# A hybrid decoder trunk on one core: embedding projections moved between mixer and MLP, two first tiles in token halves instead of four, TensorE's order there written by hand

## The chip, the cores and the metric

The kernel runs on one core of one Trainium2 chip. The metric is device time in microseconds (us) of one execution. The engines of the core are TensorE (PE, with its weight loads as PEld), VectorE (DVE), ScalarE (ACT), GpSimd (POOL, all but unused here) and the sync engine (SP), which issues the DMAs.

## The reference, cut to what matters

512 tokens of 1024 features run through two layers. A layer is a token mixer (Mamba-2 SSD in layer 0, HGRN2 in layer 1), a squared-ReLU MLP and a gated embedding; the first two are added to a scaled input and normalized.

```python
def sq_relu_mlp(h, w1, w2):
    a = jax.nn.relu(h @ w1)
    return (a * a) @ w2
...
        h = layer_norm(DEEPNORM_ALPHA * x + mix, ln_g[i, 0], ln_b[i, 0])
        h = layer_norm(DEEPNORM_ALPHA * h + sq_relu_mlp(h, mlp_w1[i], mlp_w2[i]), ln_g[i, 1], ln_b[i, 1])
        x = h + jax.nn.sigmoid(h @ ple_w_gate[i]) * (p[i] @ ple_w_proj[i])
```

`mix` is the output of the layer's mixer, which ends in a product with its output weights. p has 256 features per token and layer, so the embedding projection p @ ple_w_proj (wp in the kernel) is a quarter of the gate's matmul h @ ple_w_gate (wg), and it depends on neither h nor the mixer.

## The kernel before, in words

**Arithmetic.** Everything is float32, done in three passes: each operand is split into a rounded high part and the rest (`whi`, `wlo` for weights: a ScalarE cast and a VectorE subtraction, `split`, L110 and L112), and `mm3` issues high x high, high x low and low x high (L116, L117, L118) into one PSUM bank. Weights come in units of 128x1024 (512 KB) through three `raw` buffers; their loads stand on the sync queue.

**Tiles.** The 512 tokens are four chunks of 128. The residual stream `acc` lies in SBUF with tokens on partitions; projections need features on partitions, so each chunk is normalized, transposed by TensorE (`transpose_split`, L230: four transposes into bank pt, four into pm), copied by ScalarE (high part, L235) and VectorE (low part, L236).

**Order.** Python code issues the work, and a scheduler orders each engine's line by priorities; `tc.high_priority` moves a piece forward. Inside `tc.manual_schedule` TensorE's line is as the code is written. Each engine takes up its line in order, and the engines meet at semaphores.

**Mixer's end.** `out_project` multiplies the mixer's output by the last four weight units, chunk by chunk, two parts of 12 matmuls per chunk (one for each 512 output features; a part in the timeline is one bank `pj`). VectorE evicts each part into `acc` (L250 in layer 0, L252 in layer 1), and behind a chunk's second part stand its norm (`after`, L204 to L221: statistics, L220 subtracts the mean, L221 scales) and its transposes (`turned`). In layer 0 the eviction needs a scale per token: squares of the mixer's output are added up (`ss`), and `rms_group` sums them over features by small matmuls against ones (L721), a root and a reciprocal. In layer 1, HGRN's last two heads go through an output norm ahead of out_project: ScalarE squares sums of the core's result (L1117, L1120), VectorE scales it (L1122, L1126), TensorE transposes it (L1135, one group pt and one pm), ScalarE and VectorE split it (L1136, L1137). Out_project's first inner products need the heads before; the last ones need these.

**MLP.** `mlp_and_gate` runs five periods: T is a tile of 128 hidden features (24 matmuls, ReLU and square on ScalarE), Q a block product with w2 in Strassen's form (sums of w2 units, L323 to L329). The first period is eight T. In its first four tiles the first 256 tokens are multiplied for all four tiles before the second 256, so that the third and fourth chunk's norms have time. The last period is seven Q; behind its parts stand the second norm and the first chunk's transposes.

**Gates.** The rest of `mlp_and_gate` goes through two halves of 512 output features and four chunks each. In the first half all four chunks' projections p @ wp are made first (6 matmuls each, four banks), with turned(1) among them; then each chunk's gate (24 matmuls), a sigmoid on ScalarE, the product with the projection from PSUM (L486) and the addition to acc (L489). turned(2) and turned(3) stand inside the first and second chunk's gate. In the second half each chunk's projection stands in front of its gate.

Of the kernel before, what the change touches and what calls it, by code (L numbers as in the profile page):

```python
# [31 lines left out]
PERIODS = ("TTTTTTTT",) + 3 * ("TTQTQTQTQTQTQTQ",) + ("QQQQQQQ",)  # L32
# [9 lines left out]
def trunk(ctx: ExitStack, tc, a):  # L42
# [215 lines left out]
    def out_project(w, xs, first, after=None, turned=None, sums=None, scale=None):  # L258


        if after is not None:
            units = [unit(w[i]) for i in range(4)]
            for c in range(NCH):
                for h in range(2):
                    out_part(units[2 * h : 2 * h + 2], 4, xs, c, h, first, scale, True, sums)
                after(c)
                turned(c)
# [114 lines left out]
    def mlp_and_gate(layer, h_s, last):  # L382
# [4 lines left out]
        def hidden(g):  # L387
# [5 lines left out]
            for p in range(2):  # L393
                tiles = [4 * (2 * g + r) + 2 * p + i for r in range(2) for i in range(2)]
                us = []
                if g == p == 0:
                    for m in tiles:
                        us.append((unit(w1[m]), bank(psj, "pj")))
                        project(us[-1][0], h_s, us[-1][1], tok=slice(0, 256))
                zs = []  # L400
                for r in range(2):
                    z = mk(w4, [P, 2, T], "ab"[r])
                    for i in range(2):
                        if us:
                            u, ps = us[2 * r + i]
# [11 lines left out]

        for g, period in enumerate(PERIODS):
            if g < 4:
                tiles = hidden(g)  # L420
            if g > 0:
                if g == 4:
                    h_s, after, turned, sums = norm(2 * layer + 1)
                    p_s = (mk(w4, [P, 2, T], "a", F32R), mk(w4, [P, 2, T], "b", F32R))
                    praw = mk(raws, [P, 1024], "raw")
                    nc.sync.dma_start(praw, a[f"pT_{layer}"].rearrange("p k t -> p (k t)"))
                    praw = praw.rearrange("p (k t) -> p k t", k=2)
                    nc.scalar.copy(p_s[0], praw)
                    nc.vector.tensor_sub(p_s[1], praw, f32(p_s[0]))
# [19 lines left out]
        pps = {}  # L449

        def proj(c, pu):

            pp = pps[c] = bank(*((psj, "pj") if c > 1 and pps else (psy, "py%d" % (c % 2))))
            for k in range(2):
                ks = slice(k * 512, (k + 1) * 512)
                mm3(pp, p_s[0][:, k, c * P : (c + 1) * P], p_s[1][:, k, c * P : (c + 1) * P], pu[0][:, ks], pu[1][:, ks], k == 0, k == 1)

        for h in range(2):
            pu = unit(a[f"wp_{layer}"][h])
            gu = [unit(a[f"wg_{layer}"][4 * h + j]) for j in range(4)]  # L460
            for c in range(NCH):
                sl = slice(c * P, (c + 1) * P)
                if h == c == 0:
                    for i in range(NCH):
                        proj(i, pu)
                        if i == 1:
                            turned(1)
                if h == 1:
                    proj(c, pu)
# [813 lines left out]
```

## Time and profile before

| | |
|---|---|
| median of 3 runs | 1422.53 us (1421.46 to 1422.73) |
| profiled execution, its own time | 1422.3 us |
| its span, first to last instruction | 1420.5 us |
| mean granted TensorE clock | 1.000 |
| TensorE busy | 1413.6 us, 8143 matmul records |
| VectorE busy | 1025.4 us (72%) |
| ScalarE busy | 744.4 us (52%) |
| DMA | 174.83 MB, mean 123 GB/s |

In the page's list of engines each busy time is followed by its share of the span and the number of instructions. A timeline row gives the start in the span, the duration, the engine, the line of the code, the operation and its tiles (out<-in, shape; xN groups N that follow one another), and in brackets an idle time of the engine just before, with what ended it. Matmul rows overlap: the next one starts before the last one ends. In the list of waits a row says which instruction waited for which, the time in all, how often, and the longest.

### The profile page before, as it was taken

The page shows a single profiled execution, that of the slowest core. Times are in us where ns is not written, and L with a number is a line of the kernel's source. Part 1 is how long each engine was busy: PE and PEld are TensorE (multiplying, and loading weights), DVE is VectorE, ACT ScalarE, POOL GpSimd, SP SyncE. Part 2 cuts the span into 40 slices and gives each one's busy share as a digit, 9 for nine tenths or more (in the row PEclk, how much of TensorE's full clock was granted, in tenths as well). Part 3 has the DMA queues.
Part 4 walks back from the last instruction along what each step waited for, and adds up shares of the span by engine and source line. Part 5 has one row for each costly group of instructions (what it writes and reads, how often), then busy time and mean ns, then how long its engine had stood idle before and what let it go on. Part 6 is the DMA issues. An engine that isn't in the chain of part 4 may idle for free.

```text
span 1420.5 us, 20454 instructions
## 1 busy us (share of the span) xinstructions
PE 1413.6 (100%) x8143; PEld 1182.3 (83%) x8143; DVE 1025.4 (72%) x1713; ACT 744.4 (52%) x1089; POOL 1.6 (0%) x9
## 2 busy tenths in 40 slices
PE   9999999999999999999999999999999999999998
PEld 7888888888888888888888888888898888888887
DVE  7987777778967667677963774776785867667873
ACT  7776656664265454545543446465454544544641
POOL 0000000000000000000000000000000000000000
PEclk9999999999999999999999999999999999999999
DMA  8343333233433444442422222222163444444231
GB/s 292 127 145 108 113 118 101 95 104 124 158 119 127 156 133 149 134 148 104 149 90 91 92 92 72 90 90 76 60 238 104 148 147 135 149 133 163 89 119 45
DMA packets 48960, 174.83 MB, mean 123 GB/s; under 512 B 5728, under 2 KB 6368, under 8 KB 48736
## 3 DMA queue, kind: packets, MB, share of 16 engines
q1 hardware_dynamic: 48864, 173.52, 35.9%
q8 instruction: 64, 1.05, 0.3%
q14 instruction: 32, 0.26, 0.1%
HBM read 171.34 MB, written 2.16 MB: 122 GB/s over the span
## 4 chain that ended last, share of the span: by engine, by line
PE 96%; DVE 2%; DMA 1%; ACT 0%; issue 0%; SPq 0%
PE pj L116 25%; PE pj L118 25%; PE pj L117 25%; PE py L116 5%; PE py L118 5%; PE py L117 5%; PE py L687 1%; PE py L942 1%; PE pm L669 1%; PE py L689 1%; PE pt L635 0%; PE pt L230 0%; DMA acc<-in_xw 0%; PE pm L230 0%; DVE wlo L112 0%; DVE b L236 0%
## 5 line engine op out<-in xcount | busy, mean ns | idle before, releaser
L110 ACT CAST whi<-raw 128x1024 fp32r<-128x1024 f32 x226 | 237.1, 1050 | 377.8 <-PE pj L117 264.6
L112 DVE TENSOR_TENSOR wlo<-raw,whi 128x1024 fp32r<-128x1024 f32 x226 | 274.3, 1220 | 159.1 <-ACT whi L110 155.0
L116 PE MATMUL pj<-b,whi 128*128 128x512 f32 (+1 forms) x1008 | 381.5, 379 | 0.2 <-ACT b L235 0.2
L117 PE MATMUL pj<-b,whi 128*128 128x512 f32 (+1 forms) x1008 | 379.4, 376 | 0.7 <-DVE b L236 0.7
L118 PE MATMUL pj<-b,wlo 128*128 128x512 f32 (+1 forms) x1008 | 378.9, 376 | 0.0
L118 PE MATMUL pj<-whi,b 128*128 128x512 f32 (+1 forms) x592 | 229.5, 388 | 0.0
L116 PE MATMUL pj<-whi,b 128*128 128x512 f32 (+1 forms) x584 | 229.3, 393 | 0.0
L117 PE MATMUL pj<-wlo,b 128*128 128x512 f32 (+1 forms) x584 | 226.1, 387 | 0.0
L116 PEld LDWEIGHTS pj<-b,whi 128*128 128x128 f32 x1008 | 189.5, 188 | 36.2 <-issue 1.7
L118 PEld LDWEIGHTS pj<-b,wlo 128*128 128x128 f32 x1008 | 189.8, 188 | 34.7
L117 PEld LDWEIGHTS pj<-b,whi 128*128 128x128 f32 x1008 | 189.8, 188 | 34.6 <-DVE b L236 0.9
L118 PEld LDWEIGHTS pj<-whi,b 128*128 128x128 f32 x592 | 111.3, 188 | 22.9 <-DVE b L1137 0.2
L116 PEld LDWEIGHTS pj<-whi,b 128*128 128x128 f32 x584 | 109.8, 188 | 22.7 <-ACT k L871 0.5
L117 PEld LDWEIGHTS pj<-wlo,b 128*128 128x128 f32 x584 | 109.8, 188 | 21.2
L110 ACT CAST whi<-r 128x1024 fp32r<-128x1024 f32 x64 | 67.4, 1053 | 63.8 <-PE pj L118 35.6
L112 DVE TENSOR_TENSOR wlo<-r,whi 128x1024 fp32r<-128x1024 f32 x64 | 78.0, 1219 | 22.2 <-ACT whi L110 22.0
L118 PE MATMUL py<-whi,b 128*128 128x512 f32 x216 | 84.2, 390 | 0.0
L117 PE MATMUL py<-wlo,b 128*128 128x512 f32 x192 | 74.8, 389 | 0.0
L116 PE MATMUL py<-whi,b 128*128 128x512 f32 x192 | 74.4, 389 | 0.0
L573 DVE SCALAR_TENSOR_TENSOR cv<-pj,cst,cv 128x509 f32<-128x509 f32 (+2 forms) x66 | 49.0, 742 | 8.7 <-ACT cv L570 8.4
L118 PEld LDWEIGHTS py<-whi,b 128*128 128x128 f32 x216 | 40.5, 188 | 8.5
L116 PEld LDWEIGHTS py<-whi,b 128*128 128x128 f32 x192 | 36.1, 188 | 7.6
(321 smaller groups left out, 1816.0 us busy)
## 6 DMA issues: line engine op xcount, KB each, us to landing
raw<-in_w SPq DMA_DIRECT2D x112, 512.0 KB, 3.2
r<-in_w SPq DMA_DIRECT2D x64, 512.0 KB, 3.5
raw<-in_wssd SPq DMA_DIRECT2D x38, 512.0 KB, 3.7
a<-csd SPq DMA_DIRECT2D x16, 512.0 KB, 3.5
raw<-in_wso SPq DMA_DIRECT2D x16, 512.0 KB, 3.4
raw<-in_wg SPq DMA_DIRECT2D x16, 512.0 KB, 3.4
raw<-in_whvg SPq DMA_DIRECT2D x16, 512.0 KB, 3.3
raw<-in_whq SPq DMA_DIRECT2D x16, 512.0 KB, 3.4
```

The costliest lines, as they stand in the source:

```text
L110: nc.scalar.copy(hi[:, :n], f)
L112: nc.vector.tensor_sub(lo[:, :n], f, f32(hi[:, :n]))
L116: nc.tensor.matmul(out, sh, mh, start=start, stop=False, **kw)
L117: nc.tensor.matmul(out, sh, ml, start=False, stop=False, **kw)
L118: nc.tensor.matmul(out, sl, mh, start=False, stop=stop, **kw)
L573: nc.vector.scalar_tensor_tensor(cv[:, d:], ps[:, : T - d], convw[:, i, k : k + 1], cv[:, d:], ALU.mult, ALU.add)
L669: nc.tensor.matmul(pst_[:, c * P : (c + 1) * P], btok[:, c, :], xw[:, c].rearrange("p h q -> p (h q)"), start=True, stop=True)
L687: nc.tensor.matmul(yd[64 * r : 64 * r + 64, sl], xdt[:, c, r, :], m[:, r, sl], start=True, stop=c == 0)
L689: nc.tensor.matmul(yd[64 * r : 64 * r + 64, sl], pv[:, c - 1, r, :], ecs[:, r, (c - 1) * P : c * P], start=False, stop=True,)
L942: nc.tensor.matmul(ps[r][32 * b : 32 * b + 32, base + n * c : base + n * c + n], kk[r][:, ts], moving(r, 4 * c + b), start=True, stop=True,)
```

## The change

- A new function `embed` computes all eight projections of a layer (two feature halves, four chunks, 6 matmuls each) between out_project and the MLP. ScalarE copies each bank to SBUF (`blk`), and two DMAs of 1 MB per layer store them to DRAM (`ple`). The gates read them back in four loads per layer. The loads of p and wp have a high priority.
- The transposes of chunks 2 and 3 stand later: turned(0) and turned(1) come behind the first part of chunks 2 and 3 in out_project, turned(2) between embed's two halves, and turned(3) behind the first half tile of the MLP.
- Two tiles, not four, are done in token halves. The first of the tiles' steps is taken ahead of the periods, so the first period has one T less.
- out_project of both layers, embed and the first tiles are in a manual schedule for TensorE. rms_group is called where out_project's arguments are made, so its matmuls (L732 now) stand ahead of all of out_project's.
- The gates begin without projections; the transposes of chunks 1, 2 and 3 stand inside the gates of the chunk ahead, at k = 4 of 8.

```diff
-PERIODS = ("TTTTTTTT",) + 3 * ("TTQTQTQTQTQTQTQ",) + ("QQQQQQQ",)
+PERIODS = ("TTTTTTT",) + 3 * ("TTQTQTQTQTQTQTQ",) + ("QQQQQQQ",)
...
                     out_part(units[2 * h : 2 * h + 2], 4, xs, c, h, first, scale, True, sums)
+                    if h == 0 and c > 1:
+                        turned(c - 2)
                 after(c)
-                turned(c)
...
+    def embed(layer, turned):
+
+        with tc.high_priority(offset=2 * LEAD):
+            p_s = (mk(w4, [P, 2, T], "a", F32R), mk(w4, [P, 2, T], "b", F32R))
+            praw = mk(raws, [P, 1024], "raw")
+            nc.sync.dma_start(praw, a[f"pT_{layer}"].rearrange("p k t -> p (k t)"))
+            praw = praw.rearrange("p (k t) -> p k t", k=2)
+            nc.scalar.copy(p_s[0], praw)
+            nc.vector.tensor_sub(p_s[1], praw, f32(p_s[0]))
+        for h in range(2):
+            pu = unit(a[f"wp_{layer}"][h], 2 * LEAD)
+            out = tmp("blk", [P, NCH, T])
+            for c in range(NCH):
+                pp = bank(psj, "pj")
+                for k in range(2):
...
+                    mm3(pp, p_s[0][:, k, cs], p_s[1][:, k, cs], pu[0][:, ks], pu[1][:, ks], k == 0, k == 1)
+                nc.scalar.copy(out[:, c], pp)
+            nc.sync.dma_start(a["ple"][layer, h], out.rearrange("p c t -> p (c t)"))
+            if h == 0:
+                turned(2)
...
-                    for m in tiles:
+                    for m in tiles[:2]:
                         us.append((unit(w1[m]), bank(psj, "pj")))
                         project(us[-1][0], h_s, us[-1][1], tok=slice(0, 256))
+                        if len(us) == 1:
+                            early_turned(3)
...
+        early_turned = turned
+        tiles = hidden(0)
+        with tc.manual_schedule(engines={mybir.EngineType.PE}):
+            embed(layer, turned)
+            next(tiles)
...
+        pp = []
+        for c in range(NCH):
+            pp.append(tmp("r", [P, 2, T]))
+            nc.sync.dma_start(pp[c], a["ple"][layer, :, :, c * T : (c + 1) * T].rearrange("h p t -> p h t"))
...
-                        if h == 0 and c < 2 and k == 2:
-                            turned(c + 2)
+                        if h == 0 and c < 3 and k == 4:
+                            turned(c + 1)
...
-                    nc.vector.tensor_mul(sg[:, cs], pp[:, cs], sg[:, cs])
+                    nc.vector.tensor_mul(sg[:, cs], pp[c][:, h, cs], sg[:, cs])
...
-    out_project(a["wso"][12:16], ys[3], False, *after, scale=rms_group(3, bank(psm, "pm")))
+    with tc.manual_schedule(engines={mybir.EngineType.PE}):
+        out_project(a["wso"][12:16], ys[3], False, *after, scale=rms_group(3, bank(psm, "pm")))
```

The line of each engine shows where instructions have moved. Up to the end of layer 0's mixer TensorE's line is the same. There, in the line of before, out_project's first part (bank pj_3179) is begun behind the last part of the mixer's pieces (pj_3120), and eleven of its twelve matmuls stand ahead of the sum of squares (L721):

```order
L117 MATMUL pj_3120<-wlo_3020,b_336_1982 128x512
L118 MATMUL pj_3120<-whi_3018,b_337_1983 128x512
L116 MATMUL pj_3179<-whi_3157,b_468_2744 128x512
L117 MATMUL pj_3179<-wlo_3159,b_468_2744 128x512
L118 MATMUL pj_3179<-whi_3157,b_469_2745 128x512
```

These are its first rows, and its end is this:

```order
L117 MATMUL pj_3179<-wlo_3165,b_468_2744 128x512
L118 MATMUL pj_3179<-whi_3163,b_469_2745 128x512
L116 MATMUL pj_3179<-whi_3163,b_468_2744 128x512
L117 MATMUL pj_3179<-wlo_3165,b_468_2744 128x512
L721 MATMUL pm_3143<-ones_s_169,ss_2751 64x64 x8
L118 MATMUL pj_3179<-whi_3163,b_469_2745 128x512
```

After the change the sum of squares, now L732, stands directly behind pj_3120:

```order
L117 MATMUL pj_3120<-wlo_3020,b_336_1982 128x512
L118 MATMUL pj_3120<-whi_3018,b_337_1983 128x512
L732 MATMUL pm_3145<-ones_s_169,ss_2751 64x64 x8
L116 MATMUL pj_3181<-whi_3159,b_468_2744 128x512
L117 MATMUL pj_3181<-wlo_3161,b_468_2744 128x512
L118 MATMUL pj_3181<-whi_3159,b_469_2745 128x512
```

The eleven matmuls have moved behind it. At the same place, VectorE's line before, with the sums of squares (L715) of the last two tiles as its first and its seventh row:

```order
L715 TENSOR_TENSOR ss_2751<-ss_2751,sq_3080 128x512
L250 SCALAR_TENSOR_TENSOR acc_99<-pj_3083,ri_2741,acc_99 128x512
L705 SCALAR_TENSOR_TENSOR y_3112<-xs_2884,cst_165,py_530_3097 128x512
L706 TENSOR_TENSOR y_3112<-y_3112,sz_2955 128x512
L112 TENSOR_TENSOR wlo_3406<-raw_3402,whi_3404 128x1024
L709 SCALAR_TENSOR_TENSOR b_469_2745<-y_3112,cst_165,b_468_2744 128x512
L715 TENSOR_TENSOR ss_2751<-ss_2751,sq_3117 128x512
L250 SCALAR_TENSOR_TENSOR acc_99<-pj_3120,ri_2741,acc_99 128x512
```

And after (the line L726 is the sum):

```order
L726 TENSOR_TENSOR ss_2751<-ss_2751,sq_3080 128x512
L250 SCALAR_TENSOR_TENSOR acc_99<-pj_3083,ri_2741,acc_99 128x512
L391 TENSOR_TENSOR b_3373<-raw_3374,a_3372 128x1024
L716 SCALAR_TENSOR_TENSOR y_3112<-xs_2884,cst_165,py_530_3097 128x512
L717 TENSOR_TENSOR y_3112<-y_3112,sz_2955 128x512
L112 TENSOR_TENSOR wlo_3382<-raw_3378,whi_3380 128x1024
L720 SCALAR_TENSOR_TENSOR b_469_2745<-y_3112,cst_165,b_468_2744 128x512
L112 TENSOR_TENSOR wlo_3436<-raw_3432,whi_3434 128x1024
L726 TENSOR_TENSOR ss_2751<-ss_2751,sq_3117 128x512
L250 SCALAR_TENSOR_TENSOR acc_99<-pj_3120,ri_2741,acc_99 128x512
```

Two instructions have come ahead of the last sum: the split of p (L391) and the split of the second wp unit (L112 for wlo_3436). ScalarE's cast of that unit has likewise moved ahead of the square sq_3117, which stood in front of a cast before. Further down, VectorE's order now has the eviction of the sixth part (pj_3287) ahead of chunk 1's L220, L204 and L221; before, chunk 1's L221 stood ahead of the eviction of the sixth part.

The second place is the end of HGRN in layer 1. In TensorE's line before, 14 of out_project's matmuls (banks pj_9027, pj_9069, pj_9083) stand between the mixer's last matmul (L1113) and the first transposes (L1135), and four up to the second ones:

```order
L117 MATMUL pj_9069<-wlo_8993,b_1243_7734 128x512
L118 MATMUL pj_9069<-whi_8991,b_1244_7735 128x512
L116 MATMUL pj_9083<-whi_9003,b_1243_7734 128x512
L117 MATMUL pj_9083<-wlo_9005,b_1243_7734 128x512
L1135 MATMUL pt_8965<-cst_165,qo_8929 128x128 x4
L118 MATMUL pj_9083<-whi_9003,b_1244_7735 128x512
L116 MATMUL pj_9083<-whi_9003,b_1243_7734 128x512
L117 MATMUL pj_9083<-wlo_9005,b_1243_7734 128x512
L118 MATMUL pj_9083<-whi_9003,b_1244_7735 128x512
L1135 MATMUL pm_8966<-cst_165,qo_8930 128x128 x4
L116 MATMUL pj_9013<-whi_8997,b_1243_7734 128x512
```

After, where L1125 is the mixer's last matmul and L1147 the transposes:

```order
L1123 MATMUL pm_8906<-b_1238_7653,sc_6356 128x128
L1125 MATMUL pm_8906<-xc_8892,qt_8562 128x128
L1147 MATMUL pt_8943<-cst_165,qo_8907 128x128 x4
L116 MATMUL pj_8993<-whi_8977,b_1249_7712 128x512
L1147 MATMUL pm_8944<-cst_165,qo_8908 128x128 x4
L117 MATMUL pj_8993<-wlo_8979,b_1249_7712 128x512
L118 MATMUL pj_8993<-whi_8977,b_1250_7713 128x512
L116 MATMUL pj_8993<-whi_8977,b_1249_7712 128x512
L117 MATMUL pj_8993<-wlo_8979,b_1249_7712 128x512
```

None of out_project's matmuls is left ahead of the first transposes, and one between the two groups; what follows are the last five of the first part (pj_8993), whose inputs b_1249 and b_1250 are the split of these transposes.

The third place is the entry of layer 0's gates (layer 1's is alike). TensorE's line before, from the last product of the MLP (bank py_927) over the first chunk's transposes (pt_5868) to the projections:

```order
L117 MATMUL py_927_5611<-wlo_5854,blk_4978 128x512
L118 MATMUL py_927_5611<-whi_5852,blk_4978 128x512
L230 MATMUL pt_5868<-cst_165,acc_99 128x128 x4
L230 MATMUL pm_5869<-cst_165,acc_99 128x128 x4
L116 MATMUL pj_5986<-whi_5930,a_5568 128x512
L117 MATMUL pj_5986<-wlo_5932,a_5568 128x512
L118 MATMUL pj_5986<-whi_5930,b_5569 128x512
L116 MATMUL pj_5986<-whi_5930,a_5568 128x512
```

After, up to the first gate (bank pj_5998, with b_923 and b_925 as the high and low split of the chunk):

```order
L118 MATMUL py_943_5649<-whi_5890,blk_5022 128x512
L116 MATMUL py_943_5649<-whi_5890,blk_5022 128x512
L230 MATMUL pt_5906<-cst_165,acc_99 128x128 x4
L230 MATMUL pm_5907<-cst_165,acc_99 128x128 x4
L117 MATMUL py_943_5649<-wlo_5892,blk_5022 128x512
L118 MATMUL py_943_5649<-whi_5890,blk_5022 128x512
L116 MATMUL pj_5998<-whi_5976,b_923_5607 128x512
L117 MATMUL pj_5998<-wlo_5978,b_923_5607 128x512
L118 MATMUL pj_5998<-whi_5976,b_925_5609 128x512
```

The transposes stand two matmuls earlier, and the gate, which stood behind 24 projection matmuls, now stands behind two.

39 lines of the change are left out of this document (11 added, 28 removed).

## Prediction

> **What bounds the kernel now.** I read the shares of the engines and the chain that ended last, then the list of TensorE's waits, then the timeline at the places that the change touches.
>
> ```profile
> PE 1413.6 (100%) x8143; PEld 1182.3 (83%) x8143; DVE 1025.4 (72%) x1713; ACT 744.4 (52%) x1089; POOL 1.6 (0%) x9
> ...
> PE 96%; DVE 2%; DMA 1%; ACT 0%; issue 0%; SPq 0%
> ```
>
> The chain that ended last is TensorE for 96% of the span, and TensorE is busy for all of it. So a microsecond counts only where TensorE comes to stand: work of VectorE, ScalarE or a queue costs nothing as long as TensorE has matmuls in line.
>
> ```profile
> PE pj L117 <- DVE b L236: 0.7, 1, 0.7
> ...
> PE pj L116 <- ACT b L235: 0.2, 1, 0.2
> ```
>
> Of the few waits that the list has, these two lie where the change cuts. The timeline puts both at the entry of layer 0's MLP, where the second token halves begin right behind the last transposes (L230):
>
> ```profile
> 384.39 0.28 PE L117 MATMUL pj<-b,whi 128*128 128x256 f32 x1
> 384.51 0.28 PE L118 MATMUL pj<-b,wlo 128*128 128x256 f32 x1
> ...
> 385.06 0.60 PE L230 MATMUL pm<-cst,acc 128*128 128x128 f32 x4
> ...
> 387.31 0.39 PE L117 MATMUL pj<-b,whi 128*128 128x256 f32 x1 [0.67 <-DVE b L236]
> 387.54 0.28 PE L118 MATMUL pj<-b,wlo 128*128 128x256 f32 x1
> ```
>
> Half matmuls (256 tokens) start 0.12 us apart (384.39, 384.51). A first matmul follows a group of transposes by 0.36 (1009.29 and 1009.65 below). Without a wait the matmul at 387.54, the sixth behind the transposes, would start at 385.06 + 0.36 + 5 x 0.12 = 386.02: this stretch can give back 1.5 us.
>
> Elsewhere TensorE's line is never empty. A row shows 0.39 us for a 128x512 matmul, but they overlap; the pitch comes from starts. Eleven steps lie between 347.53 and 350.02 below: 2.49 / 11 = 0.227 us.
>
> **Term 1: layer 0, the sum of squares** (L721 before, L732 after). Now eleven matmuls of out_project stand ahead of it and cover the work on its input. After the change it stands ahead of them all.
>
> ```profile
> 347.53 0.39 PE L118 MATMUL pj<-whi,b 128*128 128x512 f32 x1
> ...
> 350.02 0.39 PE L117 MATMUL pj<-wlo,b 128*128 128x512 f32 x1
> 350.34 0.69 PE L721 MATMUL pm<-ones_s,ss 128*64 128x64 f32 x16
> ```
>
> ```profile
> 348.15 0.62 ACT L711 ACTIVATE sq<-y 128x512 f32<-128x512 f32 x1
> 348.67 1.03 ACT L110 CAST whi<-raw 128x1024 fp32r<-128x1024 f32 x1
> ```
>
> ```profile
> 347.66 1.23 DVE L112 TENSOR_TENSOR wlo<-raw,whi 128x1024 fp32r<-128x1024 f32 x1 [1.18 <-ACT whi L110]
> 348.80 0.75 DVE L709 SCALAR_TENSOR_TENSOR b<-y,cst,b 128x512 fp32r<-128x512 f32 x1
> 349.46 0.68 DVE L715 TENSOR_TENSOR ss<-ss,sq 128x512 f32<-128x512 f32 x1
> ```
>
> With one pitch behind 347.53, TensorE now reaches L732 at 347.8. VectorE's add that completes its input (L715) ended at 350.14: a wait of 2.5 at least. But the add moves too. ScalarE's cast (348.67) now stands ahead of the square (348.15); they change places, and the square ends near 349.75 instead of 348.8. VectorE has one more L112 (348.80 - 347.66 = 1.14 to the next start) ahead of the add; it waits for that cast, which ends near 349.2, and for L720 to leave at 349.5, runs to 350.65, and the add (0.68) ends at 351.3. L732 starts near 351.35: **+3.5**. Ends: 2.5, and 3.7 with the 0.2 from 350.14 to 350.34. VectorE's split of p (L391, a subtraction as long as L112) fits into its idle time before 347.66.
>
> **Term 2: layer 0, the first norms.** Chunk 1's transposes stay in out_project, behind part 7, and VectorE's order puts the eviction of part 6 ahead of chunk 1's norm: L250, a reciprocal, L220, L204, L221, then the transposes.
>
> ```profile
> 363.79 0.70 DVE L250 SCALAR_TENSOR_TENSOR acc<-pj,ri,acc 128x512 f32<-128x512 f32 x1
> ...
> 364.47 1.26 DVE L220 SCALAR_TENSOR_TENSOR acc<-acc,lnmv,a 128x1024 f32<-128x1024 f32 x1
> 365.65 0.69 DVE L204 BATCH_NORM_STATS2 lnst<-acc 128x6 f32<-128x512 f32 x1
> 366.26 1.27 DVE L221 SCALAR_TENSOR_TENSOR acc<-acc,lnrs,b 128x1024 f32<-128x1024 f32 x1
> ```
>
> From start to start these take 0.68, 1.18 and 0.61, and L221 1.27 to its end (the first holds the reciprocal): 3.74. An eviction starts 0.43 behind its last matmul (1011.70, the second of the pair at 1011.47 below, to 1012.13). Chain 4.2; TensorE has thirteen pitches for it, 2.95: wait 1.3. Chunk 0's transposes come out 0.2 late by the same count, with three sums of w2 (L324, L326, L327) in VectorE's way. **+1.5**, ends 0 and 2.5. Chunks 2 and 3 have 24 and 48 matmuls more in front (5.45 us and up), and wait for nothing.
>
> **Term 3: what goes.** The stall at the MLP's entry, **-1.5**: embed covers chunk 3's norm, and what is late next there, the split behind its transposes, has 24 half matmuls (2.9 us) as cover. And the halves: a pair costs 2 x 0.120 against 0.227, so 2 tiles x 24 pairs x 0.0135 = **-0.65** in each layer. Layer 1's entry has no stall to lose.
>
> **Term 4: layer 1, HGRN's end.** Now out_project fills TensorE while ScalarE and VectorE make the last two heads' inputs.
>
> ```profile
> 1004.64 0.48 PE L116 MATMUL pj<-whi,b 128*128 128x512 f32 x1
> ...
> 1007.93 0.60 PE L1135 MATMUL pt<-cst,qo 128*128 128x128 f32 x4
> ...
> 1009.29 0.60 PE L1135 MATMUL pm<-cst,qo 128*128 128x128 f32 x4
> 1009.65 0.48 PE L116 MATMUL pj<-whi,b 128*128 128x512 f32 x1
> ...
> 1011.47 0.62 PE L118 MATMUL pj<-whi,b 128*128 128x512 f32 x2
> 1011.93 0.39 PE L116 MATMUL pj<-whi,b 128*128 128x512 f32 x1
> ```
>
> ```profile
> 1008.57 0.69 ACT L1136 ACTIVATE b<-pt,cst 128x512 fp32r<-128x512 f32 x1 [2.18 <-PE pt L1135]
> 1009.93 0.69 ACT L1136 ACTIVATE b<-pm,cst 128x512 fp32r<-128x512 f32 x1 [0.67 <-PE pm L1135]
> ```
>
> ```profile
> 1006.42 0.20 DVE L1122 RECIPROCAL hri<-hms 128x8 f32<-128x8 f32 x1 [3.66 <-ACT hms L1120]
> ...
> 1010.65 0.75 DVE L1137 SCALAR_TENSOR_TENSOR b<-pm,cst,b 128x512 fp32r<-128x512 f32 x1 [0.61 <-ACT b L1136]
> 1012.13 0.69 DVE L252 CUSTOM_DVE_ANT_0 acc<-pj,acc 128x512 f32<-128x512 f32 x1 [0.73 <-PE pj L118]
> ```
>
> From 1004.64 there are 14 matmuls up to the transposes at 1007.93, 4 up to those at 1009.29, and 9 up to 1011.93: 27. After the change none stands ahead of the first transposes and one between the two. The chain itself stays, since it starts with TensorE's last mixer matmuls: transposes at 1007.93, copy at 1008.57, one matmul at 1009.3, the second transposes 0.3 later than now at 1009.6, their copy from 1010.25 to 1010.95, VectorE's low half to 1011.7, the part's sixth matmul at 1011.75. So at 1011.98 TensorE has 6 of these 27 behind it: 21 x 0.227 = **+4.8**. Ends: 4.0 (the second copy 0.7 sooner) and 5.3 (two pitches more). From there each part brings 12 matmuls, and chunk 1's norm has two of them as cover instead of one: no wait.
>
> **Term 5: the gates' entry, both layers.** 24 projection matmuls (5.45 us) stood between the first transposes and the gates' first matmul. Two are left.
>
> ```profile
> 703.28 0.60 PE L230 MATMUL pt<-cst,acc 128*128 128x128 f32 x4
> ...
> 706.22 0.60 PE L230 MATMUL pt<-cst,acc 128*128 128x128 f32 x4
> ```
>
> ```profile
> 706.85 0.58 ACT L235 CAST b<-pt 128x512 fp32r<-128x512 f32 x1 [1.35 <-PE pt L230]
> ```
>
> ```profile
> 701.15 0.68 DVE L358 CUSTOM_DVE_ANT_0 acc<-pj,acc 128x512 f32<-128x512 f32 x1
> ...
> 701.75 2.48 DVE L221 SCALAR_TENSOR_TENSOR acc<-acc,lnrs,b 128x1024 f32<-128x1024 f32 x2
> ...
> 705.27 0.69 DVE L236 TENSOR_TENSOR b<-pt,b 128x512 fp32r<-128x512 f32 x1
> ```
>
> The transposes move two matmuls up to 702.83, but chunk 0's L221 is done near 703.0 (half of 2.48): wait 0.2. They and two matmuls last until 704.35. The high copy comes 0.63 behind the transposes (706.22 to 706.85) and is in time. The low half (L236) has chunk 1's L221 (to 704.2) and a sum (0.6, as 701.15 to 701.75) ahead of it on VectorE, runs from 704.9 to 705.55, and the gates' third matmul, which needs it, is reached at 704.8: wait 0.8. Chunk 2's norm comes out even with its transposes, and the next group waits 0.3 for its bank. **+1.3** a layer, +2.6; ends 0 (VectorE ready) and 4 (one more L221 in front in each layer).
>
> **Costed at nothing:** eight more copies a layer on ScalarE (busy 52%), hidden behind matmuls four banks deep, and 2 MB written and read again per layer. A store waits on the sync queue for its copies and holds the loads behind it; they feed tiles that come 48 matmuls later. Without that cover one load would be late:
>
> ```profile
> raw<-in_w SPq DMA_DIRECT2D x112, 512.0 KB, 3.2
> ```
>
> 3.2 us. Fewer split groups of transposes give back 0.3.
>
> **Sum:** 3.5 + 1.5 - 1.5 - 1.3 + 4.8 + 2.6 - 0.3 = +9.3. The profiled execution took 1422.3 us (span 1420.5 and 1.8 around it), 0.2 under the median of 1422.53, so 1422.5 + 9.3 = **1431.8 us**. All low ends give +3.4 (1425.9), all high ends +12.5 (1435.0).
>
> **Rivals.** *The waits are passed (not slower).* If TensorE takes a later matmul while one waits, then L732, term 4's transposes and the gates' entry cost nothing, and only gains are left: -1.5 - 1.3 - 0.3 = -3.1, 1419.4 us. It decides from the first matmul that overtakes. Against it: at 387.31 TensorE stood 0.67 us for L236. 0.03. [...]
>
> *The waits are at their low ends (about the same).* VectorE and ScalarE gain time in each wait, and the next one shrinks: +3.4 or less, 1425 us. For it: VectorE idles 3.66 us ahead of 1006.42. Against it: terms 1 and 4 are chains that start at TensorE's own last matmul. 0.10.
>
> *The clock drops.* Two idle stretches of 3.3 to 3.5 us are longer than any in the trace. If half the clock is granted behind each for as long as it lasted, each costs half its length again: +3.4, 1435.2 us.
>
> ```profile
> 0.00:4.00 4.00, 2.95 (x14) 2.95 (x15) 0.46 (x2) 1.58 (x2) 0.54 (x7) 1.00 0.50 176
> ```
>
> Against it: the granted clock is 1.00 in the first 4 us, right after a start from rest. 0.10. [...]
>
> *Feeding comes late.* The splits of w2 and wg run behind on VectorE, and term 5 doubles or worse: 1434.5 and above. 0.05.
>
> **How the numbers follow.** The sum holds with 0.72. The range, 1425.5 to 1436, holds all its ends and the clock's case; it leaves out the first rival, half of the second and the tail of the last. About 0.2% (2.8 us) is what a measurement of this kernel can tell from no change, so slower begins at 1425.3. Faster 0.03 (first rival); same 0.07 (half of the second, 0.02 of mine); slower 0.90.
>
> **What would show it.** TensorE's waits name L732 on VectorE's L726 with 3.5 us, L1147 on L1138 with 3.3, layer 0's second transposes with 1.3, and the gates on L236 with 0.8 twice; the wait at the MLP's entry is gone. I am wrong if L732 waits under 2.5, if a matmul starts between 1004.6 and L1147 in that stretch, if the granted clock is under 1, or if the waits are these and the time is not.

## The result, and the profile after

| | before | after |
|---|---|---|
| median of 5 runs | 1422.53 us (1421.46 to 1423.33) | 1436.65 us (1436.19 to 1437.89) |
| profiled execution, its span | 1422.3, 1420.5 us | 1437.8, 1436.0 us |
| mean granted TensorE clock in the profile | 1.000 | 0.995 |

The granted clock is the share of TensorE's full pace that the profile records as granted. The change makes the kernel slower: the ratio is 1.0102 (95% interval 1.0088 to 1.0116). The predicted 1431.8 us was 4.9 short, and the measured median lies 0.65 us above the range. The direction was right, and so were most of the terms. But one case that the prediction had weighed at 0.10 happened, and one cost that it had put at nothing was 1.8 us.

The page after, TensorE's busy time and the chain that ended last:

```profile
PE 1418.8 (99%) x8047; PEld 1180.6 (82%) x8047; DVE 1025.8 (71%) x1713; ACT 758.5 (53%) x1109; POOL 1.6 (0%) x9
...
PE 94%; DVE 4%; ACT 1%; DMA 0%; issue 0%; SPq 0%; ACTq 0%
```

TensorE's busy share fell from 100% to 99%, and VectorE's share of the chain rose from 2% to 4%: TensorE now stands for VectorE. But its busy time rose too, by 5.2 us, with 96 matmul records fewer. So besides the waits there are matmuls that take longer. TensorE's waits after:

```profile
PE pt L1147 <- DVE qo L1138: 4.0, 2, 3.0
PE pm L732 <- DVE ss L726: 3.5, 1, 3.5
PE pt L230 <- DVE lnmv L205: 1.3, 1, 1.3
...
PE pj L116 <- ACT b L1148: 0.8, 1, 0.8
PE pj L118 <- DVE b L236: 0.7, 2, 0.3
...
PE pm L1147 <- DVE qo L1138: 0.4, 1, 0.4
```

L732 with 3.5, the second transposes of layer 0 (L230) with 1.3 and the last L1147 with 3.0 are there as predicted, and the wait at the MLP's entry is gone. New is that L1147 waits twice: 1.1 of its 4.0, and the 0.4 in the last row, belong to the third pair of heads, where nothing was predicted. The stretch in layer 0, out_project's begin:

```profile
348.10 0.39 PE L118 MATMUL pj<-whi,b 128*128 128x512 f32 x1
352.00 1.12 PE L732 MATMUL pm<-ones_s,ss 128*64 128x64 f32 x16 [3.51 <-DVE ss L726]
...
353.65 0.63 PE L117 MATMUL pj<-wlo,b 128*128 128x512 f32 x1
354.08 0.63 PE L118 MATMUL pj<-whi,b 128*128 128x512 f32 x1
...
357.69 0.39 PE L118 MATMUL pj<-whi,b 128*128 128x512 f32 x1
357.92 0.39 PE L116 MATMUL pj<-whi,b 128*128 128x512 f32 x1
```

No matmul overtakes the one that waits: none starts between 348.10 and 352.00. Behind the wait a matmul follows the last by 0.43 us (353.65 to 354.08), where 0.227 is usual, and by 0.23 again from 357.69 on. The same stretch in windows (behind the window and its length stand the busy times of PE, PEld, VectorE, ScalarE and GpSimd; the third figure from the right is the granted clock):

```profile
349.00:350.00 1.00, 0.00 (x0) 0.00 (x0) 1.00 (x2) 1.00 (x2) 0.00 (x0) 1.00 0.32 127
350.00:351.00 1.00, 0.00 (x0) 0.00 (x0) 1.00 (x2) 0.98 (x2) 0.00 (x0) 0.79 0.44 127
...
354.00:357.00 3.00, 3.00 (x8) 2.32 (x7) 0.00 (x0) 0.00 (x0) 0.00 (x0) 0.50 0.94 358
357.00:358.00 1.00, 1.00 (x5) 0.79 (x4) 0.00 (x0) 0.00 (x0) 0.00 (x0) 0.80 1.05 422
358.00:360.00 2.00, 2.00 (x11) 1.65 (x10) 1.85 (x3) 0.00 (x0) 0.00 (x0) 1.00 1.02 418
```

The clock drops to 0.50 while TensorE still stands (0.79 in the mean of 350 to 351) and comes back at 357.4: 6.8 us at half clock. Layer 1's wait has the same behind it:

```profile
1015.00:1016.00 1.00, 0.00 (x0) 0.00 (x0) 0.94 (x4) 0.00 (x0) 0.00 (x0) 1.00 0.00 0
...
1020.00:1023.00 3.00, 3.00 (x7) 1.85 (x7) 1.29 (x2) 0.69 (x1) 0.00 (x0) 0.50 0.00 0
1023.00:1024.00 1.00, 1.00 (x6) 0.78 (x5) 0.15 (x2) 0.00 (x0) 0.00 (x0) 1.00 0.00 0
```

Where the 15.5 us between the two profiled spans arose, from the starts of the same matmuls in both traces. 48 matmuls a layer (10.9 us) moved from the gates to embed and are taken out:

| stretch | predicted | measured |
|---|---|---|
| start to layer 0's last mixer product | 0 | +0.6 |
| layer 0, from there to the first w2 product | +3.5 + 1.5 - 1.5 - 0.65 = +2.85 | +5.4 |
| layer 0, from there to the gates' end | +1.3 less some of the 0.3 | +0.8 |
| HGRN up to its last product | 0 | +1.8 |
| layer 1, from there to the first w2 product | +4.8 - 0.65 = +4.15 | +6.0 |
| layer 1, from there to the end | +1.3 less some of the 0.3 | +0.9 |

Three rows are off: the two in which the clock drops, by 2.6 and 1.9, and HGRN, by 1.8.

### The profile page after: what moved, and what is told of

Its sections match the earlier page's. It is cut to its first block, busy times and chain, and to the rows that moved or that the text cites. A ratio compares the mean times of both kernels' runs of the same rounds, so it can differ in the third digit from the quotient of the medians.

```text
span 1436.0 us, 20303 instructions
## 1 busy us (share of the span) xinstructions
PE 1418.8 (99%) x8047; PEld 1180.6 (82%) x8047; DVE 1025.8 (71%) x1713; ACT 758.5 (53%) x1109; POOL 1.6 (0%) x9
## 4 chain that ended last, share of the span: by engine, by line
PE 94%; DVE 4%; ACT 1%; DMA 0%; issue 0%; SPq 0%; ACTq 0%
PE pj L116 25%; PE pj L118 25%; PE pj L117 25%; PE py L116 4%; PE py L117 4%; PE py L118 4%; PE py L698 1%; DVE wlo L112 1%; PE py L954 1%; PE pm L680 1%; PE py L700 1%; PE pt L646 0%; PE pt L230 0%; DVE acc L221 0%; DMA acc<-in_xw 0%; PE pm L230 0%
## 5 line engine op out<-in xcount | busy, mean ns | idle before, releaser
L112 DVE TENSOR_TENSOR wlo<-raw,whi 128x1024 fp32r<-128x1024 f32 x226 | 274.3, 1220 | 176.5 <-ACT whi L110 174.8
L116 PE MATMUL pj<-b,whi 128*128 128x512 f32 (+1 forms) x976 | 376.1, 385 | 0.0
L117 PE MATMUL pj<-b,whi 128*128 128x512 f32 (+1 forms) x976 | 373.3, 382 | 0.0
L118 PE MATMUL pj<-b,wlo 128*128 128x512 f32 (+1 forms) x976 | 373.2, 382 | 0.0
L118 PE MATMUL pj<-whi,b 128*128 128x512 f32 (+1 forms) x616 | 239.9, 389 | 0.7 <-DVE b L236 0.7
L116 PE MATMUL pj<-whi,b 128*128 128x512 f32 (+1 forms) x584 | 232.1, 397 | 0.8 <-ACT b L1148 0.8
L116 PEld LDWEIGHTS pj<-b,whi 128*128 128x128 f32 x976 | 183.4, 188 | 37.3 <-issue 1.7
L118 PEld LDWEIGHTS pj<-b,wlo 128*128 128x128 f32 x976 | 183.4, 188 | 35.7
L117 PEld LDWEIGHTS pj<-b,whi 128*128 128x128 f32 x976 | 183.5, 188 | 34.9
L118 PEld LDWEIGHTS pj<-whi,b 128*128 128x128 f32 x616 | 116.5, 189 | 25.9 <-DVE b L236 1.6
L116 PEld LDWEIGHTS pj<-whi,b 128*128 128x128 f32 x584 | 110.6, 189 | 24.8 <-ACT b L1148 1.8
L112 DVE TENSOR_TENSOR wlo<-r,whi 128x1024 fp32r<-128x1024 f32 x64 | 78.1, 1220 | 24.2 <-ACT whi L110 23.9
L116 PE MATMUL py<-whi,b 128*128 128x512 f32 x192 | 75.1, 391 | 0.0
L118 PE MATMUL py<-whi,b 128*128 128x512 f32 x192 | 74.7, 389 | 0.0
L116 PEld LDWEIGHTS py<-whi,b 128*128 128x128 f32 x192 | 36.0, 188 | 8.4 <-DVE acc L363 1.0
L118 PEld LDWEIGHTS py<-whi,b 128*128 128x128 f32 x192 | 36.0, 188 | 7.5
```

What stands on the lines that cost most here:

```text
L112: nc.vector.tensor_sub(lo[:, :n], f, f32(hi[:, :n]))
L116: nc.tensor.matmul(out, sh, mh, start=start, stop=False, **kw)
L117: nc.tensor.matmul(out, sh, ml, start=False, stop=False, **kw)
L118: nc.tensor.matmul(out, sl, mh, start=False, stop=stop, **kw)
```

## The experiments

The experiments change the kernel after, except for the fifth, which changes the kernel before. They weigh two theories. Theory A: the waits come as predicted, each of the two long ones costs a stretch at half clock besides, and HGRN's term is the feeding of embed (p's cast and split, wp's casts and splits) that the scheduler slips into HGRN's last two pairs. Rival B: the waits cost only themselves, and the rest was lost elsewhere. Times of a kernel are medians of four or five runs, and of eleven for the sum of the repairs; the kernel before took 1422.3 to 1422.7 beside them.

**1. The waits filled with unread matmuls.**

```diff
     def rms_group(g, pr):
+        for _ in range(22 if g == 3 else 0): nc.tensor.matmul(pr[:, 256:], ys[3].h(0, slice(0, P)), ys[3].h(1, slice(0, 256)), start=True, stop=True)
         for c in range(NCH):
...
         yield
+        for pad in [bank(psy, "py0")] * 12 if n == 3 else []: nc.tensor.matmul(pad, s.h(0, slice(0, P)), s.h(1), start=True, stop=True)
         pt = spare()
```

> Two groups of matmuls whose result nobody reads are added to the changed kernel, each where TensorE stood: 22 of 256 columns (2.5 us) ahead of L732 in layer 0, 12 of 512 columns (2.7 us) ahead of the last transposes of L1147 in layer 1. With them VectorE's add of squares (L726) comes out some 0.7 us sooner, since the square changes places with a cast again. Theory A (each standstill of about 3 us also costs a stretch at half clock behind it, some 2.8 us in layer 0 and 2.2 us in layer 1): L732 and L1147 come no later than before, the granted clock stays at 1.00, and the time falls by 2.8 + 2.2 + 0.7 = 5.7 us, to about 1431. Rival B (the waits cost only themselves, and the rest was lost elsewhere): it falls by 0.7 us at most, to about 1436.

Measured: 1430.73 us, ratio 1.0059 (1.0046 to 1.0071), and a granted clock of 1.000 in all five runs, where the change had 0.995 to 0.997. Layer 0, the added group, L732 and two windows of the filled kernel:

```profile
347.53 2.79 PE L729 MATMUL pm<-b 128*128 128x256 f32 x22
350.25 0.69 PE L732 MATMUL pm<-ones_s,ss 128*64 128x64 f32 x16
```

```profile
350.00:351.00 1.00, 1.00 (x20) 0.80 (x19) 1.00 (x2) 0.80 (x2) 0.00 (x0) 1.00 0.92 336
...
352.00:354.00 2.00, 2.00 (x11) 1.64 (x10) 0.07 (x1) 0.00 (x0) 0.00 (x0) 1.00 1.18 410
```

TensorE does more, and the kernel is 5.9 us faster: B falls. Layer 0's stretch got 4.5 us shorter. 0.95 of that is L732's earlier start (2.95 us behind the last mixer product, not 3.90), 1.1 the wait of L230, which VectorE's new order took to 0.1 us, and the remaining 2.5 is put down to the clock. That fits the profile after: TensorE worked through 5.4 of the 6.8 us at half clock (352.0 to 357.4), so at most 2.7 were lost. In layer 1 L1147 starts as long behind the last mixer product as before, VectorE and ScalarE keep their order, and the stretch is 1.8 us shorter. **In the profiled run the clock costs 4.3 us in all.**

**2. Layer 0's out_project in the scheduler's order.**

```diff
-    with tc.manual_schedule(engines={mybir.EngineType.PE}):
+    if True:
         out_project(a["wso"][12:16], ys[3], False, *after, scale=rms_group(3, bank(psm, "pm")))
```

> The changed kernel with layer 0's out_project no longer ordered by hand: L732 stands behind 16 matmuls of out_project (3.6 us of cover), and layer 1 is as in the change. Theory A: the wait of 3.5 us and the 2.8 us at half clock behind it both go, -6.3 us, to about 1430.3; layer 1 keeps its wait and its drop of the clock. Rival B (no cost by the clock): -3.5 us, to about 1433.1. A third outcome: the wait only moves to the first evictions (L250 needs L735's result) or to L230, and less than 3 us come back.

Measured: 1429.02 us, ratio 1.0047 (1.0034 to 1.0061), clock 0.998 to 0.999. That is 7.6 us less than the change, 1.3 more than expected: the waits at L732 and at the second transposes are both gone, and so is layer 0's half clock. Layer 1's L1147 still waits 3.0, with 6.8 us at half clock behind it.

**3. Layer 1's out_project in the scheduler's order.** The same edit at the other call.

> The changed kernel with layer 1's out_project no longer ordered by hand: 11 more of its matmuls stand ahead of the last mixer products and of the transposes of L1147. Layer 0 is as in the change. Theory A: the 4.8 us of waits and the 2.2 us at half clock behind them go, -7.0 us, to about 1429.6. Rival B (no cost by the clock): -4.8 us, to about 1431.8.

Measured: 1433.40 us, ratio 1.0073 (1.0061 to 1.0086): only 3.2 us came back. L1147's waits at the last pair are gone, but the list has a new one, in embed:

```profile
PE pj L116 <- ACT blk L401: 1.9, 1, 1.9
```

```profile
1041.05 1.05 ACT L110 CAST whi<-raw 128x1024 fp32r<-128x1024 f32 x1
1042.01 0.58 ACT L235 CAST b<-pt 128x512 fp32r<-128x512 f32 x1
...
1043.16 1.07 ACT L401 COPY blk<-pj 128x512 f32<-128x512 f32 x2
```

```profile
1042.00:1043.00 1.00, 0.00 (x0) 0.00 (x0) 1.00 (x2) 1.00 (x4) 0.00 (x0) 1.00 0.95 356
...
1045.00:1047.00 2.00, 2.00 (x6) 1.62 (x5) 1.42 (x2) 0.78 (x2) 0.00 (x0) 0.50 0.88 348
```

With TensorE earlier, all four banks of embed are full while ScalarE's line still has chunk 3's norm, a cast and a split ahead of the copies (L401). 1.9 us of wait, and again 3.4 us at half clock behind it: that is 3.6 of the missing 3.8. So the copies, "costed at nothing", were covered only because TensorE came late, and behind a wait of 1.9 us the clock halved.

**4. Smaller gaps.** As experiment 1, with 10 and 4 added matmuls in place of 22 and 12.

> The kernel with the added unread matmuls, but fewer of them: 10 of 256 columns (1.1 us) ahead of L732 and 4 of 512 columns (0.9 us) ahead of the last transposes of L1147, so that TensorE still stands some 1.5 us in layer 0 and some 2.0 us in layer 1, where it stood 3.5 and 3.0. The waits themselves end where they ended with the full filling. [...] Theory G (an idle gap of about 3 us is needed): the clock stays at 1.00 in every run, 1430.7, as with the full filling.

Measured: 1435.39 us, ratio 1.0093 (1.0078 to 1.0108), clocks 0.997 to 0.999: under 1 in every run. The time lies 4.7 us over the expected 1430.7, since the clock halved and since with so few matmuls VectorE kept the change's order in layer 0, so that the wait there was 2.2 us, and L230 waited 1.3 and 0.3 as well. In the profiled run the clock held behind layer 0's 2.2 us and halved for 3.4 us behind layer 1's 2.0 (and 0.8 soon after):

```profile
349.00:351.00 2.00, 0.23 (x2) 0.03 (x1) 2.00 (x4) 1.98 (x3) 0.00 (x0) 1.00 0.50 156
...
353.00:355.00 2.00, 2.00 (x11) 1.64 (x10) 0.00 (x0) 0.00 (x0) 0.00 (x0) 1.00 0.95 369
```

```profile
1017.00:1019.00 2.00, 1.95 (x5) 1.48 (x6) 1.01 (x2) 0.00 (x0) 0.00 (x0) 0.50 0.00 0
```

So theory G (a gap of about 3 us is needed) falls, here and by the 1.9 us of experiment 3. A gap of some 2 us had the half clock behind it in layer 1 (2.0) and not in layer 0 (2.2); what decides between them was not shown.

**5. The halves alone, in the kernel before.**

```diff
-                    for m in tiles:
+                    for m in tiles[:2]:
...
-                        if us:
-                            u, ps = us[2 * r + i]
+                        if us and r == 0:
+                            u, ps = us[i]
```

> The kernel before with the halves alone: two first tiles in halves, not four; nothing else. In it 48 half matmuls (5.7 us) less stand ahead of chunk 3's transposes, whose norm came out 0.24 us (layer 0) and 0.35 us (layer 1) ahead of them. Theory A (the projections that the change puts there are the cover that the halves gave up): TensorE stands some 5 us at the fourth transposes of each layer, with a stretch at half clock behind each, less the 0.65 us a layer that whole tiles save: +12 to +15 us, 1434 to 1438. Rival B (VectorE and ScalarE have time in hand and the norm comes sooner): within 3 us of the kernel before, 1420 to 1425.

Measured: 1432.43 us, ratio 1.0073 (1.0061 to 1.0086), +10.0 us: below theory A's 1434 to 1438, above rival B's 1425. Layer 0's fourth transposes wait as expected, layer 1's 3.4 instead of 5:

```profile
PE pt L230 <- DVE acc L221: 8.9, 2, 5.5
```

The halves are no gain that embed comes on top of; embed replaces the cover that they give up. The prediction counted both in one sum, which came out right: in the change chunk 3's transposes do not wait.

**6. p's cast later.** Layer 1's cast of p gets a scale of 1.0, which GpSimd makes from the result of the third pair of heads.

```diff
+        if n == 2:
+            one.append(mk(sm, [P, 1], "one"))
+            nc.gpsimd.tensor_scalar(one[0], f32(s.h(i))[:, 0:1], 0.0, 1.0, ALU.mult, ALU.add)
         yield
...
-            nc.scalar.copy(p_s[0], praw)
+            nc.scalar.activation(p_s[0], praw, AF.Copy, scale=one[0]) if layer else nc.scalar.copy(p_s[0], praw)
```

> The changed kernel with layer 1's cast of p (L390) held back until the third pair of heads has left its transposes, by a scale of 1.0 that GpSimd makes from the result; nothing else is moved by hand, and TensorE's order is the same. Theory A (that cast on ScalarE between the two squares of the third pair, and the evictions and the split that VectorE's order then puts ahead of L1138, are the 1.1 and 0.4 us that TensorE waits at that pair's L1147 and the extra time of HGRN's stage): -1.8 us, to about 1434.9, and only the last pair's L1147 still waits. Rival C (the cast is harmless, VectorE's line is late by itself): no change, 1436.6. Rival D (the cast only moves into the last pair's chain): the wait at the last L1147 grows by what goes here, no change either.

Measured: 1438.03 us, ratio 1.0109 (1.0095 to 1.0122): no gain. What it meant to move, in the change's trace, ScalarE, VectorE and TensorE at the third pair:

```profile
990.42 1.05 ACT L390 CAST a<-raw 128x1024 fp32r<-128x1024 f32 x1
991.37 0.27 ACT L1129 ACTIVATE qo<-pm 128x128 f32<-128x128 f32 x1
```

```profile
994.34 1.22 DVE L112 TENSOR_TENSOR wlo<-raw,whi 128x1024 fp32r<-128x1024 f32 x1
995.48 0.19 DVE L1134 RECIPROCAL hri<-hms 128x8 f32<-128x8 f32 x1
...
996.14 1.12 DVE L1138 SCALAR_TENSOR_TENSOR qo<-pt,hri,b 128x128 f32<-128x128 f32 x4
```

```profile
997.31 0.66 PE L1147 MATMUL pt<-cst,qo 128*128 128x128 f32 x4 [1.06 <-DVE qo L1138]
998.35 0.66 PE L1147 MATMUL pm<-cst,qo 128*128 128x128 f32 x4 [0.38 <-DVE qo L1138]
```

The cast stands between the squares of the pair's two halves (L1129), and the split L112 gets ahead of the reciprocal. With the cast later both waits are gone. But the displaced splits now stand in front of the last pair's L1112, and TensorE waits there, in the later kernel:

```profile
1007.39 1.23 DVE L112 TENSOR_TENSOR wlo<-raw,whi 128x1024 fp32r<-128x1024 f32 x1
1008.53 0.34 DVE L1112 SCALAR_TENSOR_TENSOR xc<-xc,tot,pt 128x128 f32<-128x128 f32 x1
```

```profile
1009.54 0.35 PE L1123 MATMUL pt<-b,sc 128*128 128x128 f32 x1 [1.13 <-DVE xc L1112]
```

So neither A nor C as written, but the rival that the wait only moves, if one place earlier than rival D had it. And the kernel lost 1.2 us in each layer's MLP, where the order of no engine had changed (experiment 9).

**7. p's cast later still,** held until the last pair's reciprocal, with the scale kept in a tile that is there already.

> The changed kernel with layer 1's cast of p alone moved, to the last pair of heads: it waits for that pair's reciprocal (L1134), by a scale of 1.0 that GpSimd writes into a tile that is there already, so that no address moves. The earlier try put it between the third and the last pair, and there it made TensorE wait 1.1 us at the last pair's L1123. ScalarE has nothing to do behind the last reciprocal until the transposes. VectorE's part of the split (L391) comes to stand between the two L1138 of the last pair, ahead of the second transposes. Theory A (the cast of p on ScalarE is the whole of what HGRN's stage lost): no wait at the third pair's L1147 nor at L1123, the stage from the scores' last products to the last mixer product as long as in the kernel before (33.8 us, where the change took 35.7), -1.9 us, and 0 to 0.7 us of it given back at the last transposes: 1434.8 to 1435.5. Rival C (VectorE's line is late by itself there): the stage keeps its 35.7 us, 1436.6.

Measured: 1437.14 us, ratio 1.0103 (1.0087 to 1.0120): no gain again. L1123 still waits 1.0 us behind the displaced splits, and the stage takes 35.2 us. Moving one piece of the feeding gives back little of it.

**8. No feeding at all in layer 1's embed.** It multiplies two tiles of zeros, and its loads, casts and splits are left out.

```diff
+            if layer: nc.gpsimd.memset(f32(p_s[0]), 0.0), nc.gpsimd.memset(f32(p_s[1]), 0.0)
...
-            pu = unit(a[f"wp_{layer}"][h], 2 * LEAD)
+            pu = [p.rearrange("p k t -> p (k t)") for p in p_s] if layer else unit(a[f"wp_{layer}"][h], 2 * LEAD)
```

> The changed kernel in which layer 1's embed is fed by nothing: it leaves out the loads, casts and splits of p and wp in layer 1 (its products are made from two tiles of zeros that GpSimd sets), so layer 1's embedding is not computed. TensorE's order and count of matmuls are unchanged, and VectorE's order around the last two pairs of heads is the one of the kernel before: two splits ahead of L1112, evictions behind L1138; where the two tries with a late cast of p had three splits ahead of L1112. Theory A (embed's feeding, p's cast at the third pair or its displaced neighbours at the last, is the whole of what HGRN's stage lost): the stage takes 33.8 us again, where the change took 35.7, TensorE waits at neither the third pair's L1147 nor L1123, and the kernel takes -1.9 us, about 1434.8. Rival C (the stage is longer for another reason, such as the hand order around it): it keeps 35 us and more, 1436.6.

Measured: 1434.48 us, ratio 1.0080 (1.0066 to 1.0094), 2.2 us less than the change. The stage's first and last product, in the change and without feeding:

```profile
977.20 0.53 PE L954 MATMUL py<-qo,k 128*32 128x56 f32 x28
...
1013.10 0.39 PE L1125 MATMUL pm<-xc,qt 128*128 128x128 f32 x2
```

```profile
976.01 0.53 PE L954 MATMUL py<-qo,k 128*32 128x56 f32 x28
...
1010.04 0.39 PE L1125 MATMUL pm<-xc,qt 128*128 128x128 f32 x2
```

35.9 us against 34.0, with the same matmuls between; before the change the stage took 34.0 as well (970.48 to 1004.49). TensorE waits at neither place. HGRN's term is the feeding as a whole: shown. Which piece of it costs how much stays open.

**9. An address moved.** The change with 8 bytes more in the pool of small tiles, used by nothing.

```diff
-    nc.gpsimd.memset(mk(pad, [P, 16], "pad"), 0.0)
+    nc.gpsimd.memset(mk(pad, [P, 16], "pad"), 0.0); nc.gpsimd.memset(mk(sm, [P, 1], "one"), 0.0)
```

> The changed kernel with one unused column of 4 bytes (two buffers, 8 bytes) put into the pool of small tiles, set once by GpSimd at the start: the order on every engine is the same, and the tiles of the later pools move to other addresses in SBUF. The kernel with the late cast of p had such a column too, and lost 1.2 us in each layer's MLP, spread evenly (a mean start to start of 228.0 ns instead of 227.0), where its order is the same. Theory A (the addresses make it): both MLP stages take 1.2 us more, 1439. Rival B (something else of that kernel, or that chip, made it): 1436.6, and MLP stages as in the changed kernel.

Measured: 1438.33 us, ratio 1.0113 (1.0099 to 1.0127), 1.7 us more than the change. Layer 0's MLP, first w2 product and the gates' first transposes, in the change and with the 8 bytes:

```profile
448.00 0.39 PE L116 MATMUL py<-whi,b 128*128 128x512 f32 x1
...
719.98 0.32 PE L230 MATMUL pt<-cst,acc 128*128 128x128 f32 x1
```

```profile
446.13 0.39 PE L116 MATMUL py<-whi,b 128*128 128x512 f32 x1
...
719.44 0.33 PE L230 MATMUL pt<-cst,acc 128*128 128x128 f32 x1
```

271.98 us against 273.31, and the same 1.3 us in layer 1; the medians differ by less than the 2.6, since the start and the half clock vary from run to run. The order on every engine is the same. Experiment 6's kernel, with such a column too, has 273.2 us in both layers, and the kernels without it, on the same chips, 271.9 to 272.2; experiment 7's, whose scale lies in a tile that is there already, has 272.0 and 272.3. So the column makes it, as theory A has it; that it does so through the addresses is argued, not shown. It plays no part in the change, whose MLPs run as fast as those before (272.2); it only spoiled experiment 6. Which tile's address it would be stays open.

**10. The repairs together.** Both out_projects in the scheduler's order, p's cast as in 7, embed's copies with a higher priority, and the gates' first low halves later.

```diff
-                nc.scalar.copy(out[:, c], pp)
+                with tc.high_priority(offset=TURN): nc.scalar.copy(out[:, c], pp)
...
+                            nc.tensor.matmul(pg[:, cs], h_s.h(k, sl), mh, start=k == 0, stop=False)
+                            nc.tensor.matmul(pg[:, cs], h_s.h(k, sl), ml, start=False, stop=False)
+                            if k == 3:
+                                for q in range(4):
+                                    nc.tensor.matmul(pg[:, cs], h_s.l(q, sl), gu[q // 2][0][:, (q % 2) * 512 + i * n : (q % 2) * 512 + (i + 1) * n], start=False, stop=False)
```

> The changed kernel with its costs taken out, one by one: both out_projects in the scheduler's order; layer 1's cast of p held until the last pair's reciprocal (by a scale of 1.0 from GpSimd, kept in a tile that is there already, so that no address moves); embed's copies from PSUM with a higher priority on ScalarE, since with out_project free the four banks of embed waited 1.9 us for a copy behind chunk 3's norm; and in the gates' first chunk the low halves' matmuls of the first four steps put behind the high ones, so that the split has 8 matmuls as cover instead of 2. Theory A (the sum of the single costs): from the 1429.0 of the kernel with layer 0 free, -7.0 in layer 1, -1.5 in HGRN, -0.9 at the gates, so about 1419.6, some 3 us under the kernel before. Rival B (new waits take their places, as that of the copies did): 1422 to 1425, no better than before. The granted clock should be 1.00.

Measured: 1421.99 us, ratio 0.9998 (0.9990 to 1.0007): all of the loss is back, and nothing more. The clock is 0.999 or 1.000 in every run. Its waits from layer 1's end of HGRN on (its lines lie 9 further down):

```profile
PE pj L116 <- ACT b L1157: 0.8, 1, 0.8
...
PE pt L1156 <- DVE qo L1147: 0.2, 1, 0.2
```

The gates give back 0.4 to 0.5 us a layer, as counted, HGRN's last products come with no wait, and layer 1 keeps 0.8 us at the last pair's copy. Against the kernel before, the two layers' entries stand at -2.1 and +0.8 and the gates at +0.5 and +0.7 in the profile: gains and losses cancel. Theory A's 1419.6 is missed by 2.4 us; the time lies at B's lower end, 1422.

## Why the prediction fell short, step by step

- **Term 1, layer 0's squares (+3.5):** 3.51. The chain was right to the last link, the changed places of cast and square included; experiment 2 takes the wait away by order alone. The low end was worked out a little too high: 350.14 less 347.8 is 2.3, not 2.5.
- **Term 2, first norms (+1.5):** 1.26 at chunk 1's transposes, as counted (1.3); chunk 0's 0.2 did not show.
- **Term 3, what goes (-1.5 and -0.65 a layer):** the stall at the MLP's entry is gone, and chunk 2 and 3's transposes wait for nothing. The halves were not timed by themselves without loss of cover.
- **Term 4, HGRN's end (+4.8):** 2.97 at the transposes (3.3 expected) and 0.78 at the copy; without the clock's 1.8 the stretch lost 4.2, where 4.15 was forecast.
- **Term 5, the gates (+1.3 a layer):** over-sized. One wait, at the third matmul, as placed, but 0.34 long, not 0.8; the other two are not there. From start to start (721.63 to 722.37) it costs 0.51 more than a pitch, most of the 0.8 in the table; for the rest the list names no wait. The rows:

```profile
721.63 0.40 PE L117 MATMUL pj<-wlo,b 128*128 128x512 f32 x1
722.37 0.50 PE L118 MATMUL pj<-whi,b 128*128 128x512 f32 x1 [0.34 <-DVE b L236]
```

- **Costed at nothing:** wrong for embed's feeding in layer 1. "VectorE's split of p (L391, a subtraction as long as L112) fits into its idle time" was looked at in layer 0 alone. In layer 1 the high priority puts 1 us of ScalarE and a split of VectorE into a chain on which TensorE waits: +1.8. The eight copies were hidden only behind the other losses (experiment 3).
- **The failed step** is the third rival, "the clock drops", put at 0.10 and outside the sum. Its mechanism happened: behind both waits in the profiled run, and with a granted clock under 1 in all five runs, which the prediction had named as a sign of being wrong. Its size, half of 3.3 to 3.5 each, +3.4, was also short: in the profile 4.3 by experiment 1, since the half clock lasted 6.8 us behind each wait.
- **The evidence against that rival** was misread. The window of the first 4 us prints a clock of 1.00, but its matmuls ran at half pace: 14 of 128x128 take 2.95 us there, 0.21 each, and in steady work two of that shape take 0.22 from start to start (1012.43 to 1012.65 in the change), 0.11 each. Experiment 3's trace has it with 128x512 matmuls, where the window from 5.40 to 6.40 prints 1.00 too:

```profile
5.48 1.05 PE L530 MATMUL py<-b,wlo 128*128 128x512 f32 x2
6.34 0.91 PE L532 MATMUL py<-b,whi 128*128 128x512 f32 x2
```

Two of them take 0.86 us, 0.43 each, the pace at half clock; in the change's trace such matmuls follow each other by 0.23 from 6.58 to 7.72. So in these traces TensorE's first matmuls took about twice what later ones took (0.21 for 0.11, 0.43 for 0.23), and the granted clock of 1.00 printed there does not show it. The pitch of the matmuls would have.

The prediction's high ends add up to +12.4, not the +12.5 that it gives; the forecast does not rest on them. With the steps above, 9.3 + 4.3 (clock) + 1.8 (HGRN) - 0.6 (the gates' two rows: 1.7 for 2.6 - 0.3) - 0.2 (term 2) + 0.6 (start) = 15.2, of 15.5 between the profiled spans. Between the medians it is 14.1: three of the five executions had less of the half clock (0.996 and 0.997, where the profiled one had 0.995).

Shorter waits than the 3.3 to 3.5 us that the third rival had in view had the half clock behind them as well: 1.9 us in experiment 3, and 2.0 with 0.8 soon after in experiment 4.

## What to carry to other kernels

A wait that a new order gives to TensorE can cost more than its own length. Here the half clock stood behind waits of 1.9, 2.0 (with 0.8 soon after), 3.0 and 3.5 us, for 3.41 or 6.83 us; each 3.41 us of it costs at most 1.7 us, an estimate from the granted 0.50 (for 6.83 us, 1.8 and 2.5 came out by experiment 1). Ask first of all what can stand in the gap. When work moves, its feeding (loads, casts, splits) moves with it: follow it on every engine and in each layer by itself, and see whose chain it now stands in. A hand-written order gives up the cover that a scheduler had found; write by hand only the stretch that it got wrong.

## What the runs showed of the chip

- The half clock lasted 3.41 or 6.83 us. Added up over windows of 0.5 us, its time at L732 is 6.83 us in the change and 3.41 in experiments 3, 6 and 8, with the same wait of 3.5 us; at layer 1's L1147 it is 6.83 in experiment 2, with a wait of 3.0. It started in the middle of a standstill (at 350.6 in the change, where TensorE stood from 348.5 to 352.0) or behind it (at 353.1 in experiment 6, where TensorE had stood from 348.1 to 351.6). What sets its start and its length was not shown.
- Waits of 1.1 and 1.3 us (the change) and one of 2.2 (experiment 4) had no half clock behind them; waits of 1.9 (experiment 3), 2.0 with 0.8 soon after (experiment 4), 3.0 and 3.5 (the change) had. So the length of a wait alone did not settle it in these runs.
- At half clock a 128x512 matmul follows the last by 0.427 us (354.08 to 356.64 in the change holds six of them); at a granted clock of 1.00 by 0.227 (347.53 to 350.02 before the change holds eleven).
- In the two kernels with a tile of 8 bytes per partition more (experiments 9 and 6) a stage in which no wait of TensorE is listed took 0.5% longer: 1.3 us in 272, and 1.2.
